# The first products of a two-layer encoder: halved first weights, an early function table, the distance table among the k tiles, other banks

## The chip, the cores and the metric

The kernel runs on one core of a Trainium2 chip. The metric is the time of one execution on the device in microseconds (us). Before the change it took 1289.71 us, the median of three runs (1287.42 to 1290.88).

## The reference

The kernel computes a two-layer encoder over one sequence of 512 tokens with 1024 features. In each layer four kinds of attention run side by side on the normed input, each with four heads of 64: neighborhood (a), differential with two maps of 32 features (b), dilated (c) and latent (d). Their outputs are joined, projected and added, and a gated FFN of 2816 follows. The groups that matter here:

```python
for l in range(DEPTH):
    h = rms_norm(x, attn_norm[l])
    proj = h @ w_in[l]
    qa, ka, va, qb, kb, vb, qc, kc, vc, cq, ckv, kr = jnp.split(proj, split_points, axis=-1)
    ...
    o_b = diff_attention(qb.reshape(B, S, H, 2, DIFF_QK_DIM), kb.reshape(B, S, H, 2, DIFF_QK_DIM),
                         vb.reshape(B, S, H, HEAD_DIM), lam, lam_init, diff_subln[l], t5_diff)
    o_c = dilated_attention(qc.reshape(B, S, H, HEAD_DIM), kc.reshape(B, S, H, HEAD_DIM),
                            vc.reshape(B, S, H, HEAD_DIM), t5_dil)
    ...
    x = x + mix @ w_o[l]
    h = rms_norm(x, ffn_norm[l])
    x = x + (jax.nn.silu(h @ w_gate[l]) * (h @ w_up[l])) @ w_down[l]
return rms_norm(x, final_norm)
```

`diff_attention` and `dilated_attention` add a bias that depends on the distance of query and key alone (`t5_bucket`); it comes from one small table for both.

## The kernel before

Everything is float32. Each product is made from two float32r parts of each operand, a high part (a rounded copy, `whi`, `h[:, 0]`) and a low part (what is left, `wlo`, `h[:, 1]`), as three products: high by high, high by low, low by high. The features lie on the 128 partitions in eight k tiles (`KD`), the 512 tokens along the free dimension. The row factor of the norm is not applied to x: the products are made of x times the gain, and their results are scaled by the row factor (`rb` as a row, `rc` as a column) when they leave PSUM.

**The start** (`tile_encoder`, L107 to L127). ScalarE's queue sends the gains (`gn`) and the weights of the first k tile (`raw_f`), SP's queue sends x and the other weights, k tile by k tile; these weights hold for each k tile the values (256 columns), keys and queries (128 each) of the differential heads of pair 0. TensorE runs `WARM` = 12 products of a tile of ones, and then `p_first`. `first_inputs` writes, tile by tile, the high and low parts: ScalarE makes the high part of h and of the weights (VectorE that of the first weights), VectorE the low parts, ScalarE the squares, VectorE their sum `ssq`. Instructions on ScalarE and VectorE are held in the written order (`turn`). ScalarE's function table is loaded ahead of its first activation.

**`p_first`** (L459 to L484) runs the eight k tiles. In each, three times (high-high, high-low, low-high): a key product and a query product of 512 columns into two banks, and four value products of 256 columns into two `acc` banks. Ahead of the last k tile stands the mean square (`rms_column`: four products with one column into the bank of tag `sm`, one step on VectorE, a power on GpSimd). Behind it come four transposes that spread the row factor into a `sm` bank (`spread_rows`), and ScalarE copies it out. PSUM has these tags: `acc` two banks, `sc` (scores) two, `tp` (transposes) two, `sm` one, `pv` one. The first keys and queries lie in the `sc` banks.

**The distance table** (`distance_table`, L318 to L332). Two plain float32 products of the table with a one-hot matrix (32 rows, 8 columns out) go into the `sm` bank, VectorE finishes each (`tbs`), and SP's queue stores it to DRAM (`tb`). Each head's bias tile `t` is loaded back from there, 448 KB; the softmax of the differential heads reads it.

**The order.** The work between the heads is a list of pieces (`ORDER`), run as filler between the steps of the heads, at rates per step (`RATES`). The piece `f` is `p_first`, `t` the distance table, `s` the stacking of pair 0 (32 copies of 64 KB through SP's queue, `sb<-kbn`, `sb<-qbn`), `1q1` the queries of differential pair 1 (`p_b`, slab `qb`), `v2` the values of the dilated heads (`v_c`, slabs `vca` and `vcb`), and so on. A slab is loaded into a ring of four raw tiles, its high part is copied by ScalarE (or another engine by the table `ENG`), its low part subtracted by GpSimd or VectorE; there are two tiles each of high and low parts. A scheduler then orders each engine's instructions by its own model of their durations, within the limits that `issue_after` sets.

Of the kernel before, what the change touches and what calls it, by code (L numbers as in the profile page):

```python
# [18 lines left out]
P = 128  # L19
# [21 lines left out]
ORDER = 'f t s 1q1 v2 1k1 2q0 l0 2k0 2k1 l1 kr nq 2q1 nqr l2 nk nkr qr 3r00 3q0 v3 3k1 3q1 v00 3k0 v01 o01 0k0 3r01 3r10 3r11 vt1 0q1 ab 0q0 vt0 0k1 o00 o10 o11 o12 o13 o2'  # L41
# [10 lines left out]
NPT = 2  # L52

# [9 lines left out]
def tile_encoder(ctx, tc, xT, gains, lamv, w_in, w_kr, w_d, w_o0, w_o1, w_o2, w_gu, w_dn,  # L63
# [43 lines left out]
    nc.scalar.dma_start(gn, gains)  # L107
    x, _ = res_tiles("in")
    wfirst = []
    for k in range(KD):  # L110
        if k % 2 == 0:
            t = wts.tile([P, 2, 512], F32, tag="raw", name=f"raw_f{k}", bufs=RAW)
        nc.sync.dma_start(x(k), xT[:, k, :])
        (nc.sync if k else nc.scalar).dma_start(t[:, k % 2, :], w_in[0, IN_B + k // 2, :, 512 * (k % 2) : 512 * (k % 2) + 512])
        wfirst.append(t[:, k % 2, :])
# [7 lines left out]
    nc.vector.memset(ones, 1.0)  # L123
    nc.vector.memset(mhalf, -0.5)
# [95 lines left out]
    def first_inputs(x, raws, nm):  # L220
# [9 lines left out]
        for k in range(KD):  # L230
# [7 lines left out]
            if k == 0:  # L238
                turn("V", lambda: nc.vector.tensor_copy(whi, raws[k]))
            else:  # L240
                turn("A", lambda: nc.scalar.copy(whi, raws[k]))
# [26 lines left out]
    def spread_rows(r, nm, n, dst):  # L268

        pt = stat_bank(f"rows_{nm}")
        if n > 1:
            rep = cst.tile([P, S], F32, tag="sq", name=f"rep_{nm}", bufs=2)
            rep = rep.rearrange("p (c h d) -> p c h d", c=4, h=n)
            nc.vector.tensor_copy(rep, r.rearrange("p (h c) -> p c h", h=n).unsqueeze(3).to_broadcast([P, 4, n, P // n]))
        for c in range(4):
            col = r[:, c : c + 1].to_broadcast([P, P]) if n == 1 else rep[:, c].rearrange("p h d -> p (h d)")
            nc.tensor.transpose(pt[:, c * P : (c + 1) * P], col, ident)
        nc.scalar.copy(dst, pt)  # L280

    def rms_rows(r, nm):

        bc = cst.tile([P, S], F32, tag="bc", name=f"bc_{nm}", bufs=3)
        spread_rows(r, nm, 1, bc)
        return bc
# [33 lines left out]
    def distance_table():  # L320
# [5 lines left out]
        for i in range(2):  # L326
            pt = stat_bank(f"t5_{i}")
# [17 lines left out]
    def attention(l, xsrc, x, hs, ssq, pl, nar):  # L345
# [95 lines left out]
        def p_norm_rows():  # L441
            g["rb"] = rms_rows(g["rc"], f"at{l}")
            yield 0.0

        def p_table():
            distance_table()
            small_tables()
            yield 8.0
# [7 lines left out]
        def p_b(p, j, bank=None):  # L456
            pt = yield from in_tile(IN_B + 2 + 2 * p + j, f"{'qk'[j]}b{p}", bank)
            if "rb" not in g:
                yield from p_norm_rows()  # L459
            b_tile(p, j, pt)  # L460

        def p_first():
# [3 lines left out]
            pkq = [score_bank(f"ip_{n}b0{l}") for n in "kq"]  # L466
            for k in range(KD):
                if k == KD - 1:
                    g["rc"] = rms_column([ssq], D, f"at{l}")
                    yield from p_norm_rows()  # L470
                whi, wlo = wfirst[k]
                for i, (a, w) in enumerate(((0, whi), (1, whi), (0, wlo))):
                    at, end = k == 0 and i == 0, k == KD - 1 and i == 2
                    for j, pt in enumerate(pkq):
                        nc.tensor.matmul(pt, w[:, 256 + P * j : 384 + P * j], hs[k][:, a, :], start=at, stop=end)
                        yield 1.0
                    for c in range(4):
                        o = pts[c // 2][:, (c % 2) * 256 : (c % 2) * 256 + 256]
                        nc.tensor.matmul(o, hs[k][:, a, c * P : (c + 1) * P], w[:, :256], start=at and c % 2 == 0,
                                         stop=end and c % 2 == 1, skip_group_check=True)  # L480
                        yield 0.5
            for j in range(2):
# [511 lines left out]
        def chain():  # L994
# [9 lines left out]
            "t": lambda: l == 0 and piece(p_table),  # L1004
# [15 lines left out]
        for p in range(2):  # L1020
            for j in range(2):
                if p:
                    make[f"1{'qk'[j]}1"] = lambda j=j: piece(p_b, 1, j)
# [336 lines left out]
```

## Time and profile before

| what | value |
|---|---|
| median of three runs | 1289.71 us (1287.42, 1289.71, 1290.88) |
| the profiled execution: its own time | 1289.56 us |
| its span, first to last instruction | 1287.7 us |
| TensorE busy | 1268.1 us, 98% |
| VectorE, ScalarE, GpSimd busy | 53%, 46%, 36% |
| mean granted clock | 0.996 of full speed |
| HBM read and written | 119.01 MB and 4.23 MB |

The profile is of one execution. PE is TensorE's products, PEld its weight loads, DVE VectorE, ACT ScalarE, POOL GpSimd, SP the queue that issues most loads. An instruction's row gives its start, its length, its line in the kernel, the tile it writes and those it reads. Times in brackets are idle time of that engine just ahead of the instruction, with what ended it. The granted clock is TensorE's share of full speed. A float32 product appears as two records. The rows of TensorE overlap, since a product drains while the next one streams.

### The profile page before, as it was taken

The page shows a single profiled execution, that of the slowest core. Times are in us where ns is not written, and L with a number is a line of the kernel's source. Part 1 is how long each engine was busy: PE and PEld are TensorE (multiplying, and loading weights), DVE is VectorE, ACT ScalarE, POOL GpSimd, SP SyncE. Part 2 cuts the span into 40 slices and gives each one's busy share as a digit, 9 for nine tenths or more (in the row PEclk, how much of TensorE's full clock was granted, in tenths as well). Part 3 has the DMA queues.
Part 4 walks back from the last instruction along what each step waited for, and adds up shares of the span by engine and source line. Part 5 has one row for each costly group of instructions (what it writes and reads, how often), then busy time and mean ns, then how long its engine had stood idle before and what let it go on. Part 6 is the DMA issues. An engine that isn't in the chain of part 4 may idle for free.

```text
span 1287.7 us, 17099 instructions
## 1 busy us (share of the span) xinstructions
PE 1268.1 (98%) x6362; PEld 1067.2 (83%) x6362; DVE 678.9 (53%) x1172; ACT 586.0 (46%) x1016; POOL 458.7 (36%) x365
## 2 busy tenths in 40 slices
PE   9999999999999999999999999999999999999997
PEld 8788888888888888888898788888888888888886
DVE  6588856655444444333237787565654444442232
ACT  5377966854332223222216778676533322233230
POOL 1276785643111111000246469756421111110000
PEclk9999999999999999999999999999999999999998
DMA  5563432222222222333346334322222222233331
GB/s 194 166 179 87 136 105 81 66 82 98 98 98 94 93 93 93 112 110 110 118 132 181 113 91 121 105 89 66 82 98 98 98 94 94 94 92 102 90 90 66
DMA packets 50915, 135.63 MB, mean 105 GB/s; under 512 B 7896, under 2 KB 12760, under 8 KB 50832
## 3 DMA queue, kind: packets, MB, share of 16 engines
q1 hardware_dynamic: 50544, 134.25, 33.4%
q8 instruction: 50, 0.82, 0.3%
q10 hardware_dynamic: 288, 0.29, 0.1%
q14 instruction: 33, 0.27, 0.1%
HBM read 119.01 MB, written 4.23 MB: 96 GB/s over the span
## 4 chain that ended last, share of the span: by engine, by line
PE 88%; DVE 5%; DMA 2%; issue 2%; ACT 2%; SPq 1%; POOL 0%; POOLq 0%; DVEq 0%; ACTq 0%
PE gu L181 12%; PE gu L183 12%; PE gu L186 12%; PE dn L186 6%; PE dn L181 6%; PE dn L183 6%; PE tp L887 2%; PE wo L186 2%; PE gu L176 2%; PE wo L183 2%; PE wo L181 1%; PE pv L900 1%; PE pv L899 1%; DVE tl L142 1%; PE sc L396 1%
## 5 line engine op out<-in xcount | busy, mean ns | idle before, releaser
L181 PE MATMUL gu<-h_f,whi_gu 128*128 128x512 f32 x672 | 261.9, 390 | 0.0
L183 PE MATMUL gu<-h_f,whi_gu 128*128 128x512 f32 x672 | 261.7, 389 | 0.0
L1151 POOL TENSOR_TENSOR u<-u,th 128x512 f32<-128x512 f32 x44 | 90.3, 2053 | 358.2 <-DVE u L1149 339.2
L186 PE MATMUL gu<-h_f,wlo_gu 128*128 128x512 f32 x672 | 166.0, 389 | 0.0
L181 PEld LDWEIGHTS gu<-h_f,whi_gu 128*128 128x128 f32 x672 | 126.1, 188 | 26.8 <-ACT whi_gu L137 0.7
L186 PEld LDWEIGHTS gu<-h_f,wlo_gu 128*128 128x128 f32 x672 | 126.1, 188 | 26.2
L183 PEld LDWEIGHTS gu<-h_f,whi_gu 128*128 128x128 f32 x672 | 126.2, 188 | 26.1
L137 ACT CAST whi_gu<-raw_gu 128x1024 fp32r<-128x1024 f32 x88 | 92.7, 1053 | 100.5 <-PE gu L183 99.8
L181 PE MATMUL dn<-act,whi_dn 128*128 128x512 f32 x330 | 128.4, 389 | 0.0
L183 PE MATMUL dn<-act,whi_dn 128*128 128x512 f32 x330 | 128.4, 389 | 0.0
L160 DVE TENSOR_TENSOR wlo_gu<-raw_gu,whi_gu 128x1024 fp32r<-128x1024 f32 x88 | 112.5, 1280 | 25.4 <-ACT whi_gu L137 16.7
L726 ACT ACTIVATE e<-e,mx 128x512 f32<-128x512 f32 (+1 forms) x128 | 85.6, 669 | 46.2 <-DVE mx L724 41.5
L160 DVE TENSOR_TENSOR wlo_dn<-raw_dn,whi_dn 128x1024 fp32r<-128x1024 f32 (+1 forms) x45 | 51.0, 1134 | 100.1 <-PE dn L186 60.5
L137 ACT CAST whi_dn<-raw_dn 128x1024 fp32r<-128x1024 f32 (+1 forms) x45 | 44.2, 982 | 127.8 <-PE dn L183 111.3
L137 ACT CAST act<-u 128x512 fp32r<-128x512 f32 x44 | 27.3, 620 | 152.2 <-POOL u L1151 152.0
L142 DVE TENSOR_TENSOR tl<-tp,th 128x512 fp32r<-128x512 f32 x112 | 75.6, 685 | 38.5 <-ACT th L137 37.9
L1149 DVE SCALAR_TENSOR_TENSOR u<-gu,bc_ff 128x512 f32<-128x512 f32 x44 | 30.4, 690 | 114.5 <-PE gu L186 114.5
L186 PE MATMUL dn<-act,wlo_dn 128*128 128x512 f32 x330 | 82.1, 389 | 0.0
L724 DVE CUSTOM_DVE_ANT_0 e<-sc,t 128x512 f32<-128x512 f32 x96 | 65.0, 684 | 31.6 <-PE tp L887 12.4
L183 PEld LDWEIGHTS dn<-act,whi_dn 128*128 128x128 f32 x330 | 62.0, 188 | 12.9
L186 PEld LDWEIGHTS dn<-act,wlo_dn 128*128 128x128 f32 x330 | 61.9, 188 | 12.9
L181 PEld LDWEIGHTS dn<-act,whi_dn 128*128 128x128 f32 x330 | 61.9, 188 | 12.8
(494 smaller groups left out, 2657.9 us busy)
## 6 DMA issues: line engine op xcount, KB each, us to landing
raw_gu<-in_w_gu_dram SPq DMA_DIRECT2D x88, 512.0 KB, 3.2
raw_dn<-in_w_dn_dram SPq DMA_DIRECT2D x32, 512.0 KB, 3.5
raw_wo<-in_w_o_dram SPq DMA_DIRECT2D x16, 512.0 KB, 3.8
t<-tb SPq DMA_DIRECT2D x16, 448.0 KB, 4.3
raw_dn<-in_w_dn_dram SPq DMA_DIRECT2D x16, 384.0 KB, 3.1
sb<-kbn SPq DMA_DIRECT2D x64, 64.0 KB, 2.0
sb<-qbn SPq DMA_DIRECT2D x64, 64.0 KB, 2.0
xin<-in_xT_dram SPq DMA_DIRECT2D x8, 256.0 KB, 5.3
```

The lines of the kernel that those rows point to most:

```text
L137: nc.scalar.copy(out, src)
L142: engine(tag, usual).tensor_tensor(out, src, hi.bitcast(F32), op=ALU.subtract)
L160: lo_eng.tensor_tensor(lo[:, c], raw[:, c], hi[:, c].bitcast(F32), op=ALU.subtract)
L176: nc.tensor.matmul(pt, w[:, k, wcol], xs[k][:, a, :], start=first and i + k == 0, stop=last and i == 2 and k == nk - 1)
L181: nc.tensor.matmul(pt, whi[:, k, wcol], xs[k][:, 0, :], start=first and k == 0, stop=False)
L183: nc.tensor.matmul(pt, whi[:, k, wcol], xs[k][:, 1, :], start=False, stop=False)
L186: nc.tensor.matmul(pt, wlo[:, k, wcol], xs[k][:, 0, :], start=False, stop=last and k == nk - 1)
L724: nc.vector.tensor_tensor_reduce(out=e, in0=sc, in1=bias, scale=1.0, scalar=BIG, op0=ALU.add, op1=ALU.min, accum_out=mx)
L726: nc.scalar.activation(e, src, AF.Exp, bias=mx, scale=-1.0, accum_out=den)
L887: u["mark"] = nc.tensor.transpose(tp[:, j * P : (j + 1) * P], u["e"][:, j * P : (j + 1) * P], ident)
L1149: nc.vector.scalar_tensor_tensor(u, pts[1], 0.5, r_bc, op0=ALU.mult, op1=ALU.mult)
L1151: nc.gpsimd.tensor_tensor(u, u, th, op=ALU.mult)
```

## The change

- The first k tile's weights come in two halves: columns 256 to 511 (keys and queries) lead ScalarE's queue, columns 0 to 255 (values) go through SP's queue between the first and the second x; the gains follow the first half on ScalarE's queue. VectorE casts the halves one after the other.
- ScalarE runs an activation of one column on the tile of ones ahead of everything, and its function table is loaded there.
- The piece `t` is gone from `ORDER`. The distance table's loads are made in `p_first`, and its two products stand at k tile 5 and within k tile 6 (`TABLE_AT`).
- The first keys and queries go to the `tp` banks instead of the `sc` banks. The queries of pair 1 in the first layer go to an `sc` bank instead of an `acc` bank, and stand behind the transposes.
- In the last k tile the key and query products stand behind the mean square, and the transposes behind the last of all products.

```diff
--- before.py
+++ after.py
@@ -38,7 +38,7 @@
 VGATE = {2: [], 3: [('pv', 1, 1)], 0: [('pv', 2, 1)]}
 NEED = {(3, 0, 0): [('out', 0, 1)], (0, 1, 1): [('out', 1, 2)]}
 HEADS = [(1, 0, 0), (1, 0, 1), (1, 1, 0), (1, 1, 1), (2, 0, 0), (2, 0, 1), (2, 1, 0), (2, 1, 1), (3, 0, 0), (3, 0, 1), (3, 1, 0), (3, 1, 1), (0, 0, 0), (0, 0, 1), (0, 1, 0), (0, 1, 1)]
-ORDER = 'f t s 1q1 v2 1k1 2q0 l0 2k0 2k1 l1 kr nq 2q1 nqr l2 nk nkr qr 3r00 3q0 v3 3k1 3q1 v00 3k0 v01 o01 0k0 3r01 3r10 3r11 vt1 0q1 ab 0q0 vt0 0k1 o00 o10 o11 o12 o13 o2'
+ORDER = 'f s 1q1 v2 1k1 2q0 l0 2k0 2k1 l1 kr nq 2q1 nqr l2 nk nkr qr 3r00 3q0 v3 3k1 3q1 v00 3k0 v01 o01 0k0 3r01 3r10 3r11 vt1 0q1 ab 0q0 vt0 0k1 o00 o10 o11 o12 o13 o2'
 NST = 10
 RAW = 4
 PRE = 0
@@ -50,6 +50,7 @@
 NAUX = 2
 NE = 4
 NPT = 2
+TABLE_AT = (5, 6)
 
 
 G_ATT, G_FFN, G_FIN, G_MQ, G_MKV, G_SUB = 0, 16, 32, 40, 44, 46
@@ -104,15 +105,21 @@
     gn = cst.tile([P, G_N], F32, name="gn")
 
 
-    nc.scalar.dma_start(gn, gains)
     x, _ = res_tiles("in")
     wfirst = []
     for k in range(KD):
         if k % 2 == 0:
             t = wts.tile([P, 2, 512], F32, tag="raw", name=f"raw_f{k}", bufs=RAW)
+        wk = w_in[0, IN_B + k // 2, :, 512 * (k % 2) : 512 * (k % 2) + 512]
+        wfirst.append(t[:, k % 2, :])
         nc.sync.dma_start(x(k), xT[:, k, :])
-        (nc.sync if k else nc.scalar).dma_start(t[:, k % 2, :], w_in[0, IN_B + k // 2, :, 512 * (k % 2) : 512 * (k % 2) + 512])
-        wfirst.append(t[:, k % 2, :])
+        if k == 0:
+
+            nc.scalar.dma_start(t[:, 0, 256:], wk[:, 256:])
+            nc.scalar.dma_start(gn, gains)
+            nc.sync.dma_start(t[:, 0, :256], wk[:, :256])
+        else:
+            nc.sync.dma_start(t[:, k % 2, :], wk)
     lv = cst.tile([P, NL, 4, 32], F32, name="lv")
     nc.sync.dma_start(lv, lamv.partition_broadcast(P))
 
@@ -121,6 +128,9 @@
     make_identity(nc, ident)
     ones = cst.tile([P, P], F32, name="ones")
     nc.vector.memset(ones, 1.0)
+
+    early = cst.tile([P, 1], F32, name="early")
+    nc.scalar.activation(early, ones[:, :1], AF.Square)
     nc.vector.memset(mhalf, -0.5)
     nc.vector.memset(hblk, 0.0)
     nc.vector.memset(hblk[0:64, 0:1], 1.0)
@@ -236,7 +246,8 @@
             whi, wlo = hi[:, k % 2, :], lo[:, k % 2, :]
             turn("A", lambda: nc.scalar.activation(h[:, 0, :], x(k), AF.Copy, scale=g))
             if k == 0:
-                turn("V", lambda: nc.vector.tensor_copy(whi, raws[k]))
+                for c in (slice(256, 512), slice(0, 256)):
+                    turn("V", lambda: nc.vector.tensor_copy(whi[:, c], raws[k][:, c]))
             else:
                 turn("A", lambda: nc.scalar.copy(whi, raws[k]))
             turn("V", lambda: nc.vector.scalar_tensor_tensor(h[:, 1, :], x(k), g, h[:, 0, :].bitcast(F32),
@@ -276,14 +287,15 @@
             nc.vector.tensor_copy(rep, r.rearrange("p (h c) -> p c h", h=n).unsqueeze(3).to_broadcast([P, 4, n, P // n]))
         for c in range(4):
             col = r[:, c : c + 1].to_broadcast([P, P]) if n == 1 else rep[:, c].rearrange("p h d -> p (h d)")
-            nc.tensor.transpose(pt[:, c * P : (c + 1) * P], col, ident)
+            mm = nc.tensor.transpose(pt[:, c * P : (c + 1) * P], col, ident)
         nc.scalar.copy(dst, pt)
-
-    def rms_rows(r, nm):
+        return mm
+
+    def rms_rows(r, nm, mark=False):
 
         bc = cst.tile([P, S], F32, tag="bc", name=f"bc_{nm}", bufs=3)
-        spread_rows(r, nm, 1, bc)
-        return bc
+        mm = spread_rows(r, nm, 1, bc)
+        return (bc, mm) if mark else bc
 
 
     warm = stat_bank("warm")
@@ -324,6 +336,7 @@
         nc.sync.dma_start(oh, onehot)
         nc.sync.dma_start(cr, crow)
         for i in range(2):
+            yield
             pt = stat_bank(f"t5_{i}")
             c = slice(i * 512, (i + 1) * 512)
             nc.tensor.matmul(pt[:8], tab, oh[:, c], start=True, stop=True)
@@ -439,13 +452,9 @@
 
 
         def p_norm_rows():
-            g["rb"] = rms_rows(g["rc"], f"at{l}")
+            g["rb"], g["rows"] = rms_rows(g["rc"], f"at{l}", True)
             yield 0.0
 
-        def p_table():
-            distance_table()
-            small_tables()
-            yield 8.0
 
         def b_tile(p, j, pt):
             sc, nm = ((-(32.0 ** -0.5), "qb"), (1.0, "kb"))[j]
@@ -453,8 +462,9 @@
             t = g[nm, p] = st_tile(f"{nm}n{p}")
             split(t[:, 0, :], t[:, 1, :], f, f"b{p}{j}")
 
-        def p_b(p, j, bank=None):
-            pt = yield from in_tile(IN_B + 2 + 2 * p + j, f"{'qk'[j]}b{p}", bank)
+        def p_b(p, j, bank=None, late=False):
+            with tc.issue_after(g["rows"].ins) if late else ExitStack():
+                pt = yield from in_tile(IN_B + 2 + 2 * p + j, f"{'qk'[j]}b{p}", bank)
             if "rb" not in g:
                 yield from p_norm_rows()
             b_tile(p, j, pt)
@@ -463,22 +473,30 @@
 
             v = g["vb"] = v_tile("b")
             pts = [acc_bank(f"v_b{l}{i}") for i in range(2)]
-            pkq = [score_bank(f"ip_{n}b0{l}") for n in "kq"]
+            pkq = [ps.tile([P, 512], F32, tag="tp", name=f"ip_{n}b0{l}", bufs=2) for n in "kq"]
+            table = distance_table()
+            next(table)
+            small_tables()
             for k in range(KD):
+                if k in TABLE_AT:
+                    with tc.issue_after(mm.ins):
+                        next(table, None)
                 if k == KD - 1:
-                    g["rc"] = rms_column([ssq], D, f"at{l}")
-                    yield from p_norm_rows()
+                    g["rc"], mark = rms_column([ssq], D, f"at{l}", mark=True)
                 whi, wlo = wfirst[k]
                 for i, (a, w) in enumerate(((0, whi), (1, whi), (0, wlo))):
                     at, end = k == 0 and i == 0, k == KD - 1 and i == 2
                     for j, pt in enumerate(pkq):
-                        nc.tensor.matmul(pt, w[:, 256 + P * j : 384 + P * j], hs[k][:, a, :], start=at, stop=end)
+                        with tc.issue_after(mark.ins) if k == KD - 1 else ExitStack():
+                            nc.tensor.matmul(pt, w[:, 256 + P * j : 384 + P * j], hs[k][:, a, :], start=at, stop=end)
                         yield 1.0
                     for c in range(4):
                         o = pts[c // 2][:, (c % 2) * 256 : (c % 2) * 256 + 256]
-                        nc.tensor.matmul(o, hs[k][:, a, c * P : (c + 1) * P], w[:, :256], start=at and c % 2 == 0,
-                                         stop=end and c % 2 == 1, skip_group_check=True)
+                        mm = nc.tensor.matmul(o, hs[k][:, a, c * P : (c + 1) * P], w[:, :256], start=at and c % 2 == 0,
+                                              stop=end and c % 2 == 1, skip_group_check=True)
                         yield 0.5
+            with tc.issue_after(mm.ins):
+                yield from p_norm_rows()
             for j in range(2):
                 b_tile(0, 1 - j, pkq[j])
             for c in range(4):
@@ -1001,7 +1019,6 @@
         make = {
             "f": lambda: [piece(p_first)] if l == 0 else [
                 piece(in_values, IN_B, "b"), *(piece(p_b, 0, j, score_bank, key=("p_b", 0, j)) for j in (1, 0))],
-            "t": lambda: l == 0 and piece(p_table),
             "s": lambda: [piece(p_stack, 0, 0, k) for k in range(4)],
             "nq": lambda: piece(p_qnorm),
             "nqr": lambda: piece(p_qnorm_rows),
@@ -1020,7 +1037,8 @@
         for p in range(2):
             for j in range(2):
                 if p:
-                    make[f"1{'qk'[j]}1"] = lambda j=j: piece(p_b, 1, j)
+                    make[f"1{'qk'[j]}1"] = lambda j=j: piece(
+                        p_b, 1, j, *[score_bank, True] * (l == 0 and j == 0), key=("p_b", 1, j))
                 make[f"2{'qk'[j]}{p}"] = lambda p=p, j=j: piece(p_c, p, j)
                 make[f"3{'qk'[j]}{p}"] = lambda p=p, j=j: piece(p_d, p, j)
                 make[f"3r{p}{j}"] = lambda p=p, j=j: piece(p_qr, p, j)
```

What moves, on three engines. TensorE around the end of `p_first`; `v_b` are the first values, `ms_at` the mean square, `rows_at` the transposes, `t` the distance table. Before:

```order
L475 MATMUL sc_ip_kb_230<-h_a_185,wlo_f_177 128x512
L475 MATMUL sc_ip_qb_231<-h_a_185,wlo_f_177 128x512
L479 MATMUL v_b_228<-wlo_f_177,h_a_185 128x256 x2
L479 MATMUL v_b_229<-wlo_f_177,h_a_185 128x256 x2
L279 MATMUL rows_at_368<-ident,rcol_at_365 128x128 x4
L329 MATMUL t_0_415<-oh,tab 8x512
L181 MATMUL ip_qb_451<-h_a_126,whi_qb_447 128x512
L183 MATMUL ip_qb_451<-h_a_126,whi_qb_447 128x512
```

With the change:

```order
L495 MATMUL v_b_233<-whi_f_180,h_a_189 128x256 x2
L495 MATMUL v_b_232<-wlo_f_181,h_a_189 128x256 x2
L495 MATMUL v_b_233<-wlo_f_181,h_a_189 128x256 x2
L271 MATMUL ms_at_379<-ones,ssq_a_128 128x1 x4
L491 MATMUL ip_kb_234<-h_a_189,whi_f_180 128x512
L491 MATMUL ip_qb_235<-h_a_189,whi_f_180 128x512
L491 MATMUL ip_kb_234<-h_a_189,whi_f_180 128x512
L491 MATMUL ip_qb_235<-h_a_189,whi_f_180 128x512
L491 MATMUL ip_kb_234<-h_a_189,wlo_f_181 128x512
L491 MATMUL ip_qb_235<-h_a_189,wlo_f_181 128x512
L290 MATMUL rows_at_407<-ident,rcol_at_386 128x128 x4
L191 MATMUL sc_ip_qb_455<-h_a_129,whi_qb_451 128x512
```

The table product has left this place; values come ahead of the mean square, keys and queries behind it, and the queries of pair 1 follow the transposes directly.

SP's queue at the same time; `raw` are slabs, `tb` the store of the table, `t` its loads for the first heads, `sb` the stacking of pair 0. Before:

```order
L147 DMA raw_vcb_527<-in_w_in_dram 128x1024
L147 DMA raw_kb_724<-in_w_in_dram 128x1024
L342 DMA sb_0_427<-kbn_0_394 32x512
L342 DMA sb_0_427<-qbn_0_399 32x512
L332 DMA tb<-tbs_417 8x512
L342 DMA sb_0_427<-qbn_0_399 32x512 x3
L342 DMA sb_0_427<-kbn_0_394 32x512 x3
L342 DMA sb_0_436<-qbn_0_399 32x512 x4
L332 DMA tb<-tbs_422 8x512
L342 DMA sb_0_436<-kbn_0_394 32x512 x4
L753 DMA t_0_0_461<-tb 128x896
```

With the change:

```order
L157 DMA raw_vca_524<-in_w_in_dram 128x1024
L345 DMA tb<-tbs_335 8x512
L157 DMA raw_vcb_531<-in_w_in_dram 128x1024
L157 DMA raw_kb_728<-in_w_in_dram 128x1024
L345 DMA tb<-tbs_358 8x512
L157 DMA raw_qc_808<-in_w_in_dram 128x1024
L771 DMA t_0_0_465<-tb 128x896
L771 DMA t_1_0_700<-tb 128x896
L157 DMA raw_cq_899<-in_w_in_dram 128x1024
L355 DMA sb_0_431<-kbn_0_415 32x512
L355 DMA sb_0_431<-qbn_0_420 32x512 x4
L355 DMA sb_0_431<-kbn_0_415 32x512 x3
```

Stores and first loads of the table, and the slabs qc and cq, stand ahead of the stacking.

ScalarE at the start. Before:

```order
L107 DMA gn<-in_gains_dram 128x48
L114 DMA raw_f_75<-in_w_in_dram 128x512
L237 ACT_TABLE_LOAD
L237 ACTIVATE h_a_126<-xin_76,gn 128x512
L237 ACTIVATE h_a_133<-xin_76,gn 128x512
```

With the change:

```order
L118 DMA raw_f_74<-in_w_in_dram 128x256
L119 DMA gn<-in_gains_dram 128x48
L133 ACT_TABLE_LOAD
L133 ACTIVATE early<-ones 128x1
L247 ACTIVATE h_a_129<-xin_75,gn 128x512
L247 ACTIVATE h_a_137<-xin_75,gn 128x512
```

Half of the first weights goes first, then the gains; the table load and the small activation have no part of x or the gains ahead of them.

## Rows read from the trace of the kernel before

**Rows 1.** The page: first line, and busy time by engine

```profile
span 1287.7 us, 17099 instructions
...
PE 1268.1 (98%) x6362; PEld 1067.2 (83%) x6362; DVE 678.9 (53%) x1172; ACT 586.0 (46%) x1016; POOL 458.7 (36%) x365
```

**Rows 2.** TensorE's waits, 41 to 330 us: who for whom, total us, times, longest

```profile
PE pv L900 <- DVE tl L142: 1.0, 2, 0.5
...
PE sc L798 <- DVE mx L724: 0.2, 1, 0.2
```

**Rows 3.** TensorE's timeline, 29 to 42 us: start, us, operation, tiles, count, [idle before]

```profile
29.89 0.60 PE L279 MATMUL rows_at<-ident,rcol_at 128*128 128x128 f32 x4
31.52 1.02 PE L329 MATMUL t<-oh,tab 32*8 32x512 f32 x2 [1.03 <-ACT bc_at L280]
33.24 0.50 PE L181 MATMUL ip_qb<-h_a,whi_qb 128*128 128x512 f32 x1 [0.69 <-DVE v_b L408]
...
40.04 1.02 PE L329 MATMUL t<-oh,tab 32*8 32x512 f32 x2
40.99 0.73 PE L186 MATMUL ip_qb<-h_a,wlo_qb 128*128 128x512 f32 x2
41.57 0.39 PE L422 MATMUL v_c<-whi_vca,h_a 128*128 128x256 f32 x2
```

**Rows 4.** 1 us each: PE, PEld, DVE, ACT, POOL busy, clock, DMA, GB/s

```profile
34.00:35.00 1.00, 1.00 (x3) 0.74 (x3) 1.00 (x3) 0.00 (x0) 0.00 (x0) 0.50 0.85 221
...
36.00:37.00 1.00, 1.00 (x4) 0.81 (x3) 0.00 (x0) 0.00 (x0) 0.00 (x0) 0.50 0.59 160
```

**Rows 5.** VectorE's timeline: the low parts of the first query slab

```profile
23.60 1.23 DVE L160 TENSOR_TENSOR wlo_qb<-raw_qb,whi_qb 128x1024 fp32r<-128x1024 f32 x1
```

**Rows 6.** TensorE's timeline: the last whole k tile, then the mean square

```profile
23.40 0.40 PE L475 MATMUL sc_ip_kb<-h_a,whi_f 128*128 128x512 f32 x1
...
26.20 0.95 PE L260 MATMUL ms_at<-ones,ssq_a 128*128 128x1 f32 x8
```

**Rows 7.** TensorE's timeline, 55 to 60 us

```profile
55.56 0.47 PE L181 MATMUL ip_kb<-h_a,whi_kb 128*128 128x512 f32 x1
...
59.30 1.52 PE L186 MATMUL ip_kb<-h_a,wlo_kb 128*128 128x512 f32 x6
```

**Rows 8.** VectorE's timeline behind the mean square

```profile
27.19 0.16 DVE L263 TENSOR_SCALAR col_at<-ms_at 128x4 f32<-128x4 f32 x1 [0.97 <-PE ms_at L260]
```

**Rows 9.** GpSimd's timeline, 27 to 33 us

```profile
27.44 1.02 POOL L265 TENSOR_TENSOR rcol_at<-col_at,mhalf 128x4 f32<-128x4 f32 x1 [26.15 <-DVE col_at L263]
30.33 2.49 POOL L160 TENSOR_TENSOR wlo_vca<-raw_vca,whi_vca 128x512 fp32r<-128x512 f32 x2 [1.87 <-ACT whi_vca L137]
```

**Rows 10.** All engines' timeline, 4 to 7 us

```profile
4.17 1.28 ACT L237 ACT_TABLE_LOAD   x1 [4.17 <-DMA xin<-in_xT_dram]
...
4.83 1.40 PEld L291 LDWEIGHTS warm<-ones 128*128 128x128 f32 x6
5.46 1.41 ACT L237 ACTIVATE h_a<-xin,gn 128x512 fp32r<-128x512 f32 x2
5.95 0.43 DVE L239 CAST whi_f<-raw_f 128x512 fp32r<-128x512 f32 x1 [1.91 <-DMA raw_f<-in_w_in_dram]
...
6.49 0.20 PEld L475 LDWEIGHTS sc_ip_kb<-h_a,whi_f 128*128 128x128 f32 x1 [0.26 <-ACT h_a L237]
```

**Rows 11.** VectorE's timeline: the first softmax

```profile
49.86 0.69 DVE L724 CUSTOM_DVE_ANT_0 e<-sc,t 128x512 f32<-128x512 f32 x1 [7.40 <-DMA t<-tb]
```

**Rows 12.** TensorE's waits, 640 to 930 us, the longest

```profile
PE sc L396 <- DVE mx L724: 1.6, 1, 1.6
```

**Rows 13.** 1 us: PE busy (count), granted clock, DMA share, GB/s

```profile
4.00:5.00 1.00, 1.00 (x6) 1.00 0.97 365
```

**Rows 14.** SP's queue: four of the stacking loads

```profile
43.02 2.40 SPq L342 DMA_DIRECT2D sb<-kbn  x4
```

**Rows 15.** The page, DMA issues: count, size of one, us to landing

```profile
sb<-qbn SPq DMA_DIRECT2D x64, 64.0 KB, 2.0
```

## Prediction

> **What bounds the kernel now.** I read the page first. TensorE is busy 1268.1 of 1287.7 us, and no other engine is above 53% [rows 1]. So the change is worth what it takes out of TensorE's row: idle time, slow products, or products themselves. The profiled execution took 1289.56 us, 1.9 more than its span; the median of the runs shown is 1289.71, so the two stand 0.15 apart, and I subtract the same gain from either. What a measurement can't tell from no change is anything within 0.3%, here 3.87 us.
>
> Next I asked whom TensorE waited for. From 41 to 330 us, the rest of the first layer's attention and the start of its FFN, four groups of waits, from 1.0 us down to 0.2, make 1.7 in all [rows 2]. That stretch has almost nothing to give. The diff speaks of the time before it, so I read TensorE's timeline from 29 us on [rows 3]. The four transposes that spread the row factors end at 29.89 + 0.60 = 30.49. Then comes 1.03 us idle: the first product of the distance table wants the bank that the transposes filled, and ScalarE must copy it out first. The table product takes until 32.55. Then 0.69 us idle: the queries of pair 1 want one of the two acc banks, which VectorE is still emptying of v_b. From 33.24 the query products run, but slowly: the granted clock is 0.50 at 34 and still at 36 us [rows 4], the 1.2 GHz level, after that thin stretch. The second table product stands in their middle, at 40.04, and the values of the dilated heads start at 41.57.
>
> **The change, part by part.** The sum runs on TensorE from its first real product to 41.57.
>
> *The idle time.* The table products leave this place, and the query products go to a score bank that nothing has used yet, with no wait ahead of them. What they need must be ready: the low parts of their weights, the last piece, were done at 23.60 + 1.23 = 24.83 [rows 5], some seven microseconds before they are wanted. Both gaps go: 1.03 + 0.69 = 1.72 us.
>
> *The table products.* In the midst of others one costs 40.99 - 40.04 = 0.95 us; alone it cost 33.24 - 0.69 - 31.52 = 1.03 [rows 3]. Both now stand among the k tiles: 1.90 instead of 1.98, so 0.08 gained. They share one bank with each other and with the mean square, so the second waits for VectorE's read of the first. Between them stand one whole k tile of 2.80 us [rows 6] and more than half of the next, over 4 us in all, which hides it; if it were not hidden, the wait would be paid in tenths.
>
> *The slow clock.* The 24 query products and the table product among them take 41.57 - 33.24 = 8.33 us. At full clock 16 such products take 59.30 - 55.56 = 3.74 us, 0.234 each [rows 7], so 24 take 5.61. What is over is 8.33 - 0.95 - 5.61 = 1.77 us. It goes if the clock stays up. The thin stretch was transposes, idle, a product with 32 rows and 8 columns, idle. Now it is transposes alone, and 24 full products follow. I take all 1.77; the other end, nothing, is a rival below.
>
> *The joint behind the transposes.* A product that follows others starts before the one ahead has drained, so a part of the 0.60 us of transposes is saved. I take 0.15, between 0 and the 0.24 by which a product of 0.47 us outlasts its 0.234 in the stream [rows 7].
>
> *Keys and queries behind the mean square.* In the last k tile the values come first, then the mean square, then the six key and query products, then the transposes. These need the power from GpSimd. The mean square ends at 26.20 + 0.95 = 27.15 [rows 6], VectorE's step at 27.35 [rows 8], the power at 28.46 [rows 9]: 1.31 us. Six products of 0.234 make 1.40. The cover holds with 0.1 us to spare; if it is missed, the price is what is missed. I cost it at nothing, 0 to 0.3 lost.
>
> *The start.* The function table load stood in wait for x and held ScalarE from 4.17 to 5.45; the first weights were cast from 5.95 to 6.38; TensorE's first real weight load came at 6.49, 0.26 us after the warm-up's last ended at 4.83 + 1.40 = 6.23 [rows 10]. The twelve warm-up products stay. So however much earlier the data come, at most 0.26 us can be won here, not the 1.28 of the table load. Without that load ScalarE can be done with the first h soon after x and the gains are there, about 4.17 + 0.7 = 4.9, and then the weights decide: half of them now leads ScalarE's queue, the other half goes before the second x. I take 0.2 of 0 to 0.26. The early table load and the tiny activation behind it lie in ScalarE's idle time up to 4.17; were that cover gone, the load would stand where it stood. Two half casts on VectorE replace one of 0.43 us; later tiles don't wait for VectorE.
>
> *SP's queue.* Both table stores, the first two table loads and the slabs qc and cq now stand ahead of the 32 stacking loads. The first softmax waited 7.40 us for the table [rows 11]; that wait goes, but it is worth nothing by itself, since TensorE worked through it. The load of cq waits until slab vca is split, and the stacking loads queue behind it: that is the slow rival.
>
> Sum: 1.72 + 0.08 + 1.77 + 0.15 + 0.2 = 3.9 us by the time the dilated values start, at about 37.7 instead of 41.57.
>
> *What comes after.* For most of the first layer's attention the scheduler has put the work in another order; FFN and second layer stand as before. The 1.7 us of waits there may go or grow. The nearest row for growth is the second layer's attention, the same work in another order: one single wait there took 1.6 us [rows 12]. I take 0.2 lost, from 1.7 gained to 3.2 lost (two such waits); it is nearest to the row of the first layer itself, whose order was as arbitrary. Forecast: 3.9 - 0.2 = 3.7 us less than 1289.71, **1286.0**.
>
> **The rivals.** *The reordered attention waits more.* For it: the first layer waits so little that a new order more likely adds than removes. Against it: products to fill with are plentiful, and the softmax work starts earlier. Two waits of 1.6 us in place of the 0.2: 1286.0 + 3.0 = 1289.0.
>
> *The halves come no earlier.* The DMA engines were 0.97 busy from 4 to 5 us, moving 365 GB/s [rows 13], and splitting a transfer may move nothing. Then the 0.2 of the start is not won: 1286.2. The Trainium skill has a rule for this in DMA: Bandwidth & Descriptors, Rules for kernel authors: loads issued by several engines share the same 16 DMA engines, so spreading them saves issue time and no more. The trace agrees that the engines were full, and no run here shows the halves. Against it: the second x no longer goes before half of these weights.
>
> *The clock falls all the same.* Mean square, six products and transposes are a thinner stretch than k tiles. Against it: the drop came after 1.72 us of idle time with a thin product between. The 1.77 stay: 1287.8.
>
> *The waits that are left go,* with softmax earlier: 1286.0 - 0.2 - 1.7 = 1284.1.
>
> *Slower: the stacking loads come too late.* GpSimd began to split vca 0.44 us after the transposes began, and took 2.49 [rows 3, 9]. Now the transposes begin at 29.89 + 1.90 - 0.2 = 31.6, so the split ends near 34.5, cq is issued, and eight stacking loads of 0.6 us each [rows 14], with 2.0 to land [rows 15], are there at about 34.5 + 0.5 + 4.8 + 2.0 = 41.8. The first score product stands behind 57 of the 96 value products, half as wide and so 0.117 us each: 37.7 + 6.7 = 44.4. So 2.6 us are to spare. Should the split be late by 4.5 us, TensorE idles 1.9, the clock falls once more (1.8), and the gain of 3.7 is gone; beyond that it is slower. Late by 9 us it is 1289.7 - 3.7 + 6.4 + 1.8 = 1294.2. Against it: GpSimd sat idle 1.87 us before that split [rows 9].
>
> **How the numbers follow.** The forecast has 0.45, about even on both sides of 1285.84, where 0.3% begins: 0.22 faster, 0.23 within. More waits 0.18 (within). Halves no earlier 0.15 (0.06 faster, 0.09 within). The clock 0.05 (within). Remaining waits gone 0.12 (faster). Late loads 0.05 (0.04 slower by over 0.3%). Faster 0.40, within 0.56, slower 0.04. The range takes in 1284.1 and 1289.0 with the start, the joint and the late power at their better or worse ends, 0.2 below and 0.6 above, and 0.7 for the scatter of a median on either side (the three runs shown lie within 3.5): 1283.2 to 1290.3. Outside are the late loads and little more.
>
> **What would show it.** In the profile after: first real product at 6.3; the two table products at about 20 and 26 us; no idle time before the first query product, which starts near 32; granted clock 1.00 from 34 to 37; the dilated values at 37.5 to 38; the first softmax near 45. The mechanism is wrong if the clock is low there or the idle time has only moved; the remainder is wrong if waits from 38 to 330 us exceed 3 us.

## The result and the profile after

The changed kernel takes 1303.38 us, the median of five runs (1301.36 to 1307.98), and the kernel before 1290.88 beside it on the same chip (1287.42 to 1293.24): a ratio of 1.0106, 95% interval 1.0090 to 1.0123. It is some 13 us slower; a gain of 3.7 was forecast, and the range ended at 1290.3.

The head of the page of the changed kernel, the lines of [rows 1]:

```profile
span 1301.3 us, 17106 instructions
...
PE 1280.9 (98%) x6362; PEld 1065.4 (82%) x6362; DVE 675.8 (52%) x1173; ACT 586.5 (45%) x1017; POOL 460.3 (35%) x365
```

TensorE runs as many products as before and is busy 12.8 us longer with them. So most of the loss is no waiting: products themselves have become longer. Before asking which, I follow the forecast from the start. TensorE's timeline of the changed kernel, 6 to 39 us, which answers to [rows 3, 6], and the first softmax on VectorE [rows 11]:

```profile
6.21 0.50 PE L491 MATMUL ip_kb<-h_a,whi_f 128*128 128x512 f32 x1 [0.80 <-ACT h_a L247]
...
25.94 1.02 PE L342 MATMUL t<-oh,tab 32*8 32x512 f32 x2
...
29.69 0.95 PE L271 MATMUL ms_at<-ones,ssq_a 128*128 128x1 f32 x8
...
32.00 0.65 PE L290 MATMUL rows_at<-ident,rcol_at 128*128 128x128 f32 x4
32.40 0.48 PE L191 MATMUL sc_ip_qb<-h_a,whi_qb 128*128 128x512 f32 x1
...
38.08 0.40 PE L435 MATMUL v_c<-whi_vca,h_a 128*128 128x256 f32 x2
...
45.16 0.69 DVE L742 CUSTOM_DVE_ANT_0 e<-sc,t 128x512 f32<-128x512 f32 x1 [6.20 <-PE sc L816]
```

Stretches of the changed kernel: from and to, length, PE busy (count), granted clock, DMA share, GB/s, as in [rows 13]:

```profile
34.00:35.00 1.00, 1.00 (x6) 1.00 0.97 362
...
36.00:37.00 1.00, 1.00 (x6) 1.00 0.65 82
```

The start does in the main what was forecast. No idle time stands behind the transposes, the clock is 1.00 where it was 0.50, the query products take 38.08 - 32.40 = 5.68 us, and the dilated values start 3.5 us earlier (at 38.08, before at 41.57).

So the time is lost later. I take five marks from each trace: the first dilated value product, the first gate or up product (tile `gu`) of each layer, the first down product (`dn`) of layer 0, and the span.

| mark, us | before | after | difference | new in this stretch |
|---|---|---|---|---|
| first `v_c` | 41.6 | 38.1 | -3.5 | -3.5 |
| first `gu`, layer 0 | 281.9 | 283.1 | +1.2 | +4.7 (attention 0) |
| first `dn`, layer 0 | 523.0 | 530.8 | +7.8 | +6.6 (gate and up 0) |
| first `gu`, layer 1 | 914.8 | 922.2 | +7.4 | -0.4 (down 0, attention 1) |
| span | 1287.7 | 1301.3 | +13.6 | +6.2 (FFN 1) |

Of the stretches that lose time, two thirds and more of the loss lie where the change edits nothing, while the gate and up products run. The costliest groups of the page (line, operation, tiles, count, then busy us and mean ns of one), first of the kernel before:

```profile
L181 PE MATMUL gu<-h_f,whi_gu 128*128 128x512 f32 x672 | 261.9, 390 | 0.0
...
L186 PE MATMUL gu<-h_f,wlo_gu 128*128 128x512 f32 x672 | 166.0, 389 | 0.0
...
L181 PE MATMUL dn<-act,whi_dn 128*128 128x512 f32 x330 | 128.4, 389 | 0.0
```

and of the changed kernel:

```profile
L191 PE MATMUL gu<-h_f,whi_gu 128*128 128x512 f32 x672 | 266.5, 397 | 0.0
...
L196 PE MATMUL gu<-h_f,wlo_gu 128*128 128x512 f32 x672 | 170.6, 396 | 0.0
...
L191 PE MATMUL dn<-act,whi_dn 128*128 128x512 f32 x330 | 128.5, 389 | 0.0
```

A gate or up product has become 6 to 7 ns longer, a down product of the same shape has not. The clock is not it. A stretch of FFN in both kernels, before first (columns as above):

```profile
330.00:480.00 150.00, 150.00 (x663) 1.00 0.29 99
```

```profile
330.00:480.00 150.00, 150.00 (x645) 1.00 0.27 95
```

TensorE is busy throughout at a granted clock of 1.00 in both. 150/663 is 226.2 ns from product to product, 150/645 is 232.6: 6.3 ns more, and 2112 such products (3 x 672 + 96) make 13.3 us.

### The profile page after: what moved, and what is told of

Its sections match the earlier page's. It is cut to its first block, busy times and chain, and to the rows that moved or that the text cites. A ratio compares the mean times of both kernels' runs of the same rounds, so it can differ in the third digit from the quotient of the medians.

```text
span 1301.3 us, 17106 instructions
## 1 busy us (share of the span) xinstructions
PE 1280.9 (98%) x6362; PEld 1065.4 (82%) x6362; DVE 675.8 (52%) x1173; ACT 586.5 (45%) x1017; POOL 460.3 (35%) x365
## 4 chain that ended last, share of the span: by engine, by line
PE 89%; DVE 4%; DMA 2%; ACT 2%; issue 2%; POOL 1%; SPq 1%; POOLq 0%; DVEq 0%; ACTq 0%
PE gu L193 12%; PE gu L196 12%; PE gu L191 12%; PE dn L196 6%; PE dn L191 6%; PE dn L193 6%; PE tp L905 2%; PE gu L186 2%; PE v_c L435 2%; PE wo L196 2%; PE wo L193 1%; PE wo L191 1%; PE pv L918 1%; PE pv L917 1%; DVE tl L152 1%
## 5 line engine op out<-in xcount | busy, mean ns | idle before, releaser
L191 PE MATMUL gu<-h_f,whi_gu 128*128 128x512 f32 x672 | 266.5, 397 | 0.0
L193 PE MATMUL gu<-h_f,whi_gu 128*128 128x512 f32 x672 | 265.7, 395 | 0.0
L196 PE MATMUL gu<-h_f,wlo_gu 128*128 128x512 f32 x672 | 170.6, 396 | 0.0
L147 ACT CAST th<-tp 128x512 fp32r<-128x512 f32 x112 | 63.8, 583 | 23.7 <-PE pv L917 16.2
L191 PEld LDWEIGHTS dn<-act,whi_dn 128*128 128x128 f32 x330 | 62.0, 188 | 12.9
L196 PEld LDWEIGHTS dn<-act,wlo_dn 128*128 128x128 f32 x330 | 62.0, 188 | 12.8
```

Of the source, the lines that this page charges most:

```text
L147: nc.scalar.copy(out, src)
L191: nc.tensor.matmul(pt, whi[:, k, wcol], xs[k][:, 0, :], start=first and k == 0, stop=False)
L193: nc.tensor.matmul(pt, whi[:, k, wcol], xs[k][:, 1, :], start=False, stop=False)
L196: nc.tensor.matmul(pt, wlo[:, k, wcol], xs[k][:, 0, :], start=False, stop=last and k == nk - 1)
```

## The experiments

**What makes the products longer.** In the list of the built program one thing differs for them: places in SBUF, the memory that the engines read. The four-byte tile `early` takes 32 bytes of pool `cst`, and every buffer behind it moves. Bytes from the start of a partition, of one buffer each:

```
            before    after
h_f          49696    49696     ahead of the tile
early            -    68128
whi_gu       98336    98368
act         127008   127040
```

Before, the buffers of h, of the weights and of `act` stood whole multiples of 512 bytes apart. Now h, the moving operand of the gate and up products (the one that streams past the loaded weights), stands 32 bytes off against their weights; the down products read `act` and `whi_dn`, which moved together. Theory: the offset of the two operands against each other sets the pace. Rivals: the other PSUM banks, or the new order. Four kernels tell them apart.

*The tile taken away,* in the changed kernel:

```diff
-    early = cst.tile([P, 1], F32, name="early")
-    nc.scalar.activation(early, ones[:, :1], AF.Square)
+    nc.scalar.activation(nlam[0], ones[:, :1], AF.Square)
```

> The changed kernel, but the early activation writes a cell that exists already, so that the four-byte tile is gone and every buffer lies where it lay before; no other instruction differs. If the tile's place is the cause (weights and h at different offsets within 64 bytes): gate and up products back at a mean of 389 to 390 ns (396 in the changed kernel), layer stretch 330 to 480 us back at 663 records, time 1287 to 1291 us, that is 13 us under the changed kernel. If the other banks or the new order of the attention slow them: 395 to 397 ns and 1303 us stay.

Measured: 1291.25 us against 1290.42 before, ratio 0.9999 (0.9988 to 1.0009); gate and up products at 389 to 390 ns, 664 in the stretch. The 13 us are the tile's place. The projections of the second attention read h and the moved weights too: TensorE is busy 267.20 us there before (641.5 to 914.8), 268.76 in the changed kernel (649.0 to 922.2), but its idle time shrinks from 6.1 to 4.4 us, which is why the table has no loss there. And what is left of the change is worth nothing: the second question, below.

*The tile alone,* in the kernel before:

```diff
     nc.vector.memset(ones, 1.0)
+    early = cst.tile([P, 1], F32, name="early")
```

> The kernel before with nothing but an unused four-byte tile declared at the place where the change declares its own. If the tile's place is the cause: gate and up products go from 389 to 396 ns and the time from 1290 to about 1303 to 1304 us, though not one instruction is new; the down products, whose weights and whose moving operand both lie behind the tile, stay at 389 ns. If banks or order are the cause: no change, 1290 us.

Measured: 1304.69 us, ratio 1.0107 (1.0094 to 1.0120). From its page:

```profile
L182 PE MATMUL gu<-h_f,whi_gu 128*128 128x512 f32 x672 | 266.2, 396 | 0.0
...
L182 PE MATMUL dn<-act,whi_dn 128*128 128x512 f32 x330 | 128.4, 389 | 0.0
```

Every engine runs the same instructions in the same order as in the kernel before. A declaration that nothing uses costs 1.1%.

*The tile sixteen times as large,* in the changed kernel:

```diff
-    early = cst.tile([P, 1], F32, name="early")
-    nc.scalar.activation(early, ones[:, :1], AF.Square)
+    early = cst.tile([P, 16], F32, name="early")
+    nc.scalar.activation(early[:, :1], ones[:, :1], AF.Square)
```

> The changed kernel with the tile made 64 bytes long, so that what lies behind it moves by 64 bytes and not by 32. If the offset within 64 bytes decides: 389 to 390 ns and 1287 to 1291 us, as without the tile. If any shift between weights and h slows them, or an offset within 128 bytes decides: 396 ns and 1303 us stay.

Measured: 1302.93 us, ratio 1.0098 (1.0083 to 1.0113), gate and up products 394 ns. The offset within 64 bytes is not what decides.

*The other pair of operands,* in the kernel before:

```diff
+        pl.tile([P, 1], F32, name=f"pad{l}")
         act = []
```

> The kernel before with an unused four-byte tile ahead of the activations of the FFN: the down products' moving operand moves by 32 bytes, their weights stay, and the gate and up products' operands both stay. If the offset of the two against each other decides: the 990 down products go from 389 to 396 ns, 6.3 ns of pace each, so about 6.2 us slower in all (1296 to 1297 us), and the gate and up products stay at 389 to 390 ns. If it is the place of the weights alone that counts: no change, 1290 us, down products 389 ns.

Measured: 1296.16 us, ratio 1.0041 (1.0026 to 1.0055), 5.7 us more; down products 394 to 396 ns, gate and up 389 to 390. The slowness has moved to the other pair, as the offset theory says. Against the weights' place alone this speaks twice: here they did not move, and in the changed kernel the down products' weights moved without harm.

*Four more offsets,* in the kernel before:

```diff
     nc.vector.memset(ones, 1.0)
+    cst.tile([P, 32], F32, name="pad_cst")
...
+                if k == 0:
+                    wts.tile([P, 8], F32, name="pad_wts")
                 lo = wts.tile([P, 2, 512], F32R, tag="wlo", name=f"wlo_f{k}", bufs=2)
...
+        pl.tile([P, 64], F32, name=f"pad{l}")
         act = []
```

> The kernel before with unused tiles of three sizes, so that weights and moving operands stand at four other offsets against each other: gate and up products at 128 bytes (high weights) and 160 (low), down products at 288 (high) and 256 (low). If only whole multiples of 512 bytes, as before, keep the pace: all four at 394 to 397 ns. If multiples of 128 do: 389 ns at 128 and 256, 395 at 160 and 288. If some offset streams better than in the kernel before, a mean under 389 ns shows it. With all four slow the time is about 1290 + 13 + 6 = 1309 us, with two slow about 1299 us.

Measured: 1310.5 us (two executions), ratio 1.0160 (1.0141 to 1.0178). Neither of the two rules expected fits: 128 is slow, and 256, which one group alone has, nearly is not. With the runs above, mean ns of a product by the distance of its two operands, in bytes beyond a multiple of 512:

| offset | 0 | 32 | 64 | 128 | 160 | 256 | 288 |
|---|---|---|---|---|---|---|---|
| ns | 389, 390 | 394 to 397 | 394 | 393, 396 | 395 | 390 | 394, 395 |

Whole multiples of 512 (the k tiles and both parts of h differ by such) run at 389 to 390, 256 nearly so, all others tried at 393 to 397. None is quicker than what the kernel before had.

Another rival moves along with the offset: other engines and transfers that use the same buffers at the same time. The traces have it. In the changed kernel 117 gate and up products run while no other engine has an instruction and no transfer is under way; they take 394 to 397 ns, and the 58 such products of the kernel before take 389. One such stretch of the changed kernel (from and to, length, then PE, PEld, DVE, ACT, POOL busy, granted clock, DMA share, GB/s):

```profile
323.10:323.60 0.50, 0.50 (x3) 0.40 (x3) 0.00 (x0) 0.00 (x0) 0.00 (x0) 1.00 0.00 0
```

What is left are TensorE's own reads: a product's, and those of the weight loads that run beside it (PEld). Why they get in each other's way, if it is that, is not shown.

**What became of the start's gain.** Without the tile, the dilated values start at 37.5 us and the first gate or up product comes at 284.3, 2.4 later than before. TensorE's idle time from 38 to 280 us is 242 - 235.53 = 6.5 us there, 2.4 before. Its waits from 41 to 330 us, where [rows 2] made 1.7:

```profile
PE tp L904 <- DVE e L821: 2.7, 2, 2.1
PE sc L408 <- DVE mx L741: 2.5, 2, 2.1
PE pv L917 <- DVE tl L151: 0.9, 2, 0.5
```

and the clock behind the second of the long ones (columns as above):

```profile
142.00:144.00 2.00, 2.00 (x11) 0.50 0.86 259
144.00:146.00 2.00, 2.00 (x8) 0.50 0.43 132
146.00:148.00 2.00, 2.00 (x8) 0.50 0.43 107
```

About 4 us of new waits and some 3 us of half clock (6 us and a part at half speed) are more than the gain. That is one execution, and not all pay for the clock: of the twelve without the tile, the four with a mean granted clock of 0.997 or 0.998 took 1286.9 to 1289.8 us, the seven with 0.993 to 0.995 took 1291.2 to 1292.7. Of the 17 of the kernel before beside them, 13 have 0.997 or more and two 0.995 or less. The two long waits, followed back through the timelines of all engines of this kernel:

```profile
86.17 0.39 SPq L546 DMA_DIRECT2D raw_kr<-in_w_kr_dram  x1
90.85 0.62 ACT L548 CAST whi_kr<-raw_kr 128x512 fp32r<-128x512 f32 x1 [3.07 <-DMA raw_kr<-in_w_kr_dram]
93.30 0.59 ACT L146 CAST th<-tp 128x512 fp32r<-128x512 f32 x1
93.92 0.69 DVE L151 TENSOR_TENSOR tl<-tp,th 128x512 fp32r<-128x512 f32 x1 [3.88 <-ACT th L146]
97.57 0.75 DVE L821 SCALAR_TENSOR_TENSOR e<-e,rd_11010w,e 128x512 f32<-128x512 f32 x1
98.47 0.63 PE L904 MATMUL tp<-ident,e 128*128 128x128 f32 x4 [2.09 <-DVE e L821]
...
138.12 1.28 POOL L585 TENSOR_TENSOR rb<-rn,ropeq 128x512 f32<-128x512 f32 x1 [2.44 <-ACT v_d L419]
139.43 0.69 DVE L586 TENSOR_TENSOR ra<-ra,rb 128x512 f32<-128x512 f32 x1 [2.01 <-POOL rb L585]
140.79 0.50 PE L408 MATMUL sc<-ks_c,qs_c 128*128 128x512 f32 x1 [2.13 <-DVE mx L741]
```

The first begins with a load: the rope key's weights are issued at 86.17, behind the stacking copies in SP's queue, and are there at 90.85. ScalarE stands before their cast, though TensorE wants them only at 98.85; `th` of the next head is queued behind it, VectorE stands for `th`, TensorE for VectorE's `e`. The changed kernel has the same row (a wait of 2.20 until 91.24, then 2.00 of TensorE). In the kernel before ScalarE came to that cast later, with its load there, and did not wait:

```profile
96.76 0.62 ACT L531 CAST whi_kr<-raw_kr 128x512 fp32r<-128x512 f32 x1
```

The second: VectorE stands in `ra` for GpSimd's `rb`, whose rotated rows SP copies until 136.3, and a softmax stands behind `ra`. In the kernel without the tile I first took the second wait off VectorE, then kept that edit and added filler ahead of the first, and then, without these two edits, took the first off ScalarE. The edits below leave out what takes the tile away.

```diff
-            engine("rq1", "P").tensor_tensor(ra, ra, rb, op=ALU.add)
+            engine("rq1" if l else "rq1_0", "P").tensor_tensor(ra, ra, rb, op=ALU.add)
```

> The change without its tile, as in the first run, and one instruction of layer 0 moved from VectorE to GpSimd: the sum of the rotated queries (ra, 0.69 us), on which VectorE stood 2.01 us for GpSimd's product rb, with the softmax of a dilated head queued behind it. If that wait made TensorE's stall of 2.13 us at 140.8 us and the clock of 0.50 from 142 to 148 us behind it: stall and slow clock go, 2.1 us and about 3.2 us, from 1291.25 to about 1286 us. If the clock falls for another reason, only the stall goes: 1289 us. If the wait only moves to another product: 1291 us.

Measured: 1289.85 us, ratio 1.0002 (0.9993 to 1.0011). A miss: the stall shrank from 2.13 to 1.02 us, but five others from 0.3 to 0.8 us came up behind it, and idle time from 38 to 280 us grew to 7.6. The half clock came all the same, behind the waits that were left there: 0.68 from 148 to 150 us and 0.50 to 152.

```diff
+EXTRA = {(0, 9): 20.0}
...
+            x = EXTRA.get((l, i), 0.0)
-            fill(rate * FR[1] / 3)
+            fill(rate * FR[1] / 3 + x)
...
-            fill(rate * FR[2] / 3)
+            fill(rate * FR[2] / 3 - x)
```

> As the run before it, and twenty more units of filler products ahead of the transposes of the tenth step in layer 0 (as many fewer behind them), so that nine products of the rope key stand between the last scores and the transposes which waited 2.09 us for VectorE's e at 98.5 us. If those waits, and not the changed start, are what took the gain away: about 2 us less again, 1283 to 1285 us, and faster than the kernel before by over 0.3%. If the filler is only missed later: as the run before it, within 1 us.

Measured: 1290.66 us, ratio 1.0005 (0.9996 to 1.0014). Another miss: nine products more stood ahead of the transposes, and they still waited 1.58 us, at 100.4. VectorE's `e` had come later too; filler doesn't mend a chain that is late at its head.

```diff
-            nc.scalar.copy(w[:, :, 0, :], raw)
+            (nc.scalar.copy if l else nc.gpsimd.tensor_copy)(w[:, :, 0, :], raw)
```

> The change without its tile, and one instruction of layer 0 moved: the cast of the rope key's weights (whi_kr, 0.62 us) goes from ScalarE to GpSimd, which subtracts the same weights right behind. On ScalarE it stood 3.07 us for its load (until 90.85 us) with the th of the next head behind it; VectorE then stood 3.88 us for that th, and TensorE's transposes 2.09 us at 98.5 us for VectorE's e. No other instruction changes its place. If the late load in ScalarE's row is what makes that stall: the stall at 98 us goes whole, about 2 us, from 1291.25 to about 1289 us. If VectorE is late by its own work: the stall stays above 1 us and the time at 1291 us.

Measured: 1287.55 us against 1289.89, ratio 0.9982 (0.9972 to 0.9992): faster than the kernel before by a little, clear of 1 but within the 0.3% that the prediction called no change. Its rows for the same place:

```profile
90.80 0.59 ACT L146 CAST th<-tp 128x512 fp32r<-128x512 f32 x1
...
91.22 0.61 POOL L548 CAST whi_kr<-raw_kr 128x512 fp32r<-128x512 f32 x1 [2.16 <-DMA raw_kr<-in_w_kr_dram]
...
96.52 0.63 PE L904 MATMUL tp<-ident,e 128*128 128x128 f32 x4 [0.38 <-DVE e L821]
```

The wait for the load is still there, but on GpSimd, with nobody behind it who matters. `th` comes 2.5 us earlier and the stall is 0.38 instead of 2.09. The first gate or up product comes at 279.6, 2.3 us earlier than in the kernel before, and nine of the eleven executions have a mean granted clock of 0.997 or more. How much of the gain is the stall and how much the clock is not separated.

Then the first and the last of these three edits together:

> Both of the single moves: whi_kr of layer 0 cast by GpSimd, and the sum of the rotated queries of layer 0 by GpSimd. If the two waits in a row (ScalarE on a load, VectorE on GpSimd behind SP's eight copies) are what took the start's gain of some 4 us away: both stalls of 2.1 us go, 1286 to 1288 us, faster than the kernel before by 0.2 to 0.3%. If the waits only move on to other instructions: 1289 to 1291 us.

Measured: 1288.07 us, ratio 0.9989 (0.9980 to 0.9998); not to be told from the run before it.

And the last one alone, in the kernel before:

> A control: the kernel before with the rope key's weights of layer 0 cast by GpSimd and nothing else edited (the scheduler also shifts some neighbours in layer 0). In the kernel before this cast waited for nothing on ScalarE. If the 2.3 us by which the mended kernel beats the kernel before come from the changed start, this one stays within 1.5 us of 1290 us, or gets slower by what the shifted neighbours cost. If the move of the cast is a gain by itself: about 1288 us.

Measured: 1290.74 us, ratio 1.0004 (0.9995 to 1.0013). The cast's move, with the neighbours that the scheduler shifts for it, is no gain by itself; it lets a part of the start's gain through.

## Why the prediction was wrong

- **Idle time, table products, clock, joint** (3.7 of the 3.9): right in mechanism, half a microsecond short. From the first product to the dilated values TensorE took 41.57 - 6.52 = 35.05 us before and 38.08 - 6.21 = 31.87 in the changed kernel, 3.2 less. The clock is 1.00, and the transposes take 32.40 - 32.00 = 0.40 of TensorE's row where they took 0.60. The rival of the late stacking loads did not come: TensorE's first wait is at 53.9 us.
- **The start** (0.2): 0.3 (first product at 6.21, before at 6.52). The bound of 0.26 was wrong: it took the end of the warm-up for fixed, but the warm-up's products ended at 6.53 before and at 5.41 in the changed kernel, and without the tile the first product came at 5.79, 0.7 earlier than before. What is waited for is now another: TensorE stood 0.80 us for ScalarE's first h, and that for the gains, which the change had put behind the first half of the weights.
- **"FFN and second layer stand as before"**: the step that failed. True of the instructions and their order, false of their operands' places. I costed the tiny activation at nothing because it lies in ScalarE's idle time; that its tile moves what is allocated behind it I did not ask. By the sum above it cost 13.3 us in the gate and up products, against 13.6 by which the whole span grew, and no rival held it.
- **"I take 0.2 lost" for the remaining waits**: mis-sized. It measured 5.4 us of waits from 41 to 330 us in the changed kernel (2.5 + 2.0 + 0.9) against 1.7, over the 3 us that the prediction had named as the sign of a wrong remainder, and a clock of 0.50 behind the first long one:

```profile
98.00:100.00 2.00, 1.13 (x7) 0.91 0.01 4
100.00:102.00 2.00, 2.00 (x6) 0.50 0.37 113
102.00:104.00 2.00, 2.00 (x8) 0.74 0.37 150
```

  My bound of two such waits (3.2 us) was a little short for the waits alone (5.4 - 1.7 = 3.7); and I left out that the clock can fall behind a long wait, though [rows 3, 4] showed just that. Without the tile these two make the change worth nothing, which is near the rival of a reordered attention (1289.0); with the late load taken off ScalarE, 2.3 of the 3.7 us are there by the medians.
- The pages bear on the step that failed. The Trainium skill (TensorE: Matmul & The Clock Gate, Step-by-step: what each phase is for) says that the loading of the next weights doesn't steal SBUF read bandwidth from the running product. The Trainium skill (SBUF — State Buffer, SBUF: two separate sides) says that on the engines' side only the port pair shared by VectorE and GpSimd makes contention. Neither gives a tile's place a price. Measured here, the same instructions in the same order run 1.1% longer with 32 bytes between, and the products are as slow where only TensorE's own reads are under way. Whether it is the weights' load that the product meets is not shown.

## What to carry to other kernels

When a change declares a buffer, however small, compare where everything behind it now lies: here products were quickest with both operands whole multiples of 512 bytes apart, and 32 bytes cost 1.1%; a scratch cell that exists already costs nothing. If groups that nobody edited get a longer mean at the same clock, look at places before order. In a new order, look on each in-order engine for an instruction that waits for a load its consumer needs much later: the work queued behind it is what pays.

## What the runs showed of the hardware that I had not expected

- A float32r product of 128x512 has a mean of 389 to 397 ns by the offset of its two operands in SBUF alone, and a pace of 226 or 233 ns (the table above).
- The longer products are there too while no other engine and no transfer is at work (394 to 397 ns in 117 of them), so TensorE's own reads are what is left to cause it.
- The same wait in the same order of instructions does not always lower the clock. The transposes at 98 us waited 2.00 us in the changed kernel, 2.09 without the tile and 2.08 with the tile of 64 bytes. The clock fell to 0.50 behind it in the changed kernel (above); in the other two, in this order, it stayed at 1.00:

```profile
100.00:102.00 2.00, 2.00 (x11) 1.00 0.61 205
```

```profile
100.00:102.00 2.00, 2.00 (x11) 1.00 0.49 131
```

  Likewise, behind 2.13 us idle at 140.8 without the tile it fell to 0.50 for six us (above), and in the kernel with the cast on GpSimd 2.49 us idle at the same product left it at 1.00:

```profile
142.00:144.00 2.00, 2.00 (x13) 1.00 0.45 142
```

  What tells them apart was not tried. One trace's clock is that of one execution.
